# Norms between attention and feed-forward: VectorE and ScalarE steps in a written order, tiles in two pairs, fewer small steps

## The chip, the core and the metric

The kernel runs on one core of one Trainium2 chip. The metric is the device time of one execution in microseconds (us). Before the change it is 681.78 us, the median of 3 runs (680.45 to 683.81).

## What is computed

One layer of a decoder on a sequence of 512 tokens of width 1024: a token mixer (differential attention and sparse attention side by side), then a SwiGLU channel mixer, with an RMSNorm before and after each. The change is about the lines in the middle, between the output projection of the mixer and the two projections `w_gate` and `w_up`:

```python
def rms_norm(x, g):
    xf = x.astype(jnp.float32)
    y = xf * lax.rsqrt(jnp.mean(xf * xf, axis=-1, keepdims=True) + NORM_EPS)
    return (y * g.astype(jnp.float32)).astype(x.dtype)
...
        mix = hybrid_mixer(h, ...)              # ends with ... @ w_out
        x = x + rms_norm(mix, attn_post_norm[l])
        h = rms_norm(x, ffn_pre_norm[l])
        f = (jax.nn.silu(h @ w_gate[l]) * (h @ w_up[l])) @ w_down[l]
        x = x + rms_norm(f, ffn_post_norm[l])
```

## The kernel before

Everything is float32 in meaning; for TensorE each operand is split into a high and a low part of type fp32r, and each product is three products (high by high, low by high, high by low). The 512 tokens are four tiles of 128 rows, the partitions; a tile's 1024 columns are two halves of 512. A PSUM tile of 128 x 512 is called a bank below.

**Up to the norms.** `mix_part` (L683) has computed the first half of the sum of the output projection into `mixp`, held in the buffers named `rope`. `mix_final` (L695) adds the second half in PSUM: tiles 0 and 1 (`mix0`, `mix1`) end with the last attention head, tiles 2 and 3 follow on TensorE at once, in banks of the tag "o" (four banks).

**The norms.** `norm_post(i, mix)` (L807) handles the norm after attention for tile i. For each half, VectorE adds the two partial sums (L811), GpSimd multiplies by the norm's weights (`u`, L812). `row_rsqrt` (L785) squares the halves on ScalarE with a running sum per row (L788), VectorE adds the two sums (L791), and `rsqrt_mean` (L126) makes the row's 1/sqrt: logarithm and exponential on ScalarE (L129, L130), then four steps of one number a row on VectorE (L131 to L138), a Newton step among them. Then VectorE adds `u` times that to the residual `x2[i]` (L815). `norm_pre(i)` (L819) norms `x2[i]` again for the feed-forward: the squares, the row's 1/sqrt, and the product with weights and 1/sqrt, for tiles 0 and 2 as a GpSimd product (L824) and a ScalarE one (L828), for tiles 1 and 3 as one VectorE instruction (L830); the string `PREE = "adad"` (L73) says which. TensorE transposes the result (L835, `trh`), ScalarE rounds it to `hth` (L838), VectorE makes the low part `htl` (L839).

**After the norms.** `ff_gate` (L890) multiplies two column blocks of `w_gate` and `w_up` by `hth` and `htl`, first for tokens 0 to 255 (tiles 0 and 1), then for tokens 256 to 511: 48 products of 256 columns for each of two blocks and each half, so 96 a half (`gu`, L897). A third block follows for all tokens (48 products of 512 columns). Each ends with Silu on ScalarE (L902) and a product on VectorE (L903). `h_sums_a`, `h_sums` and `h_split` (L856 to L881) form sums of the tiles, and `ff_prep` (L924) sums of the weights, for `ff_seven` (L956), which computes the other 19 blocks with seven half-size products each (`gw`, L917).

**Order of the work.** The program is written step by step, and a scheduler with its own model of time then orders each engine's queue; `tc.high_priority` moves a group forward, and `tc.issue_after` fixes one instruction behind another. Each engine works through its queue strictly in that order. The four `norm_post` and `norm_pre` groups are written one after the other with priorities `HP2` and `HP3`:

```python
    for i in range(NT):
        ...
        with tc.high_priority(offset=HP2 * (NT - i)):
            norm_post(i, mix if i > 1 else (mix0, mix1)[i])
        if i:
            with tc.high_priority(offset=HP3 * (NT - i + 1)):
                norm_pre(i - 1)
```

The last norm of the layer, at the end of the program, uses `row_rsqrt` too (L1239).

Of the kernel before, what the change touches and what calls it, by code (L numbers as in the profile page):

```python
# [84 lines left out]
def hybrid_block_kernel(  # L85
# [699 lines left out]
    def row_rsqrt(src, tag, also=None):  # L785
        ss = cpool.tile([P, 2], F32, tag="ss" + tag, name="ss", bufs=2)
        for c in range(2):
            act.activation(junk[tag], src[c], AF.Square, accum_out=ss[:, c:c + 1])  # L788
            if also and c == 0:
                also(c)  # L790
        dve.tensor_tensor(ss[:, 0:1], ss[:, 0:1], ss[:, 1:2], OP.add)  # L791
        r = cpool.tile([P, 1], F32, tag="rs" + tag, name="rs", bufs=2)
        rsqrt_mean(r, ss[:, 0:1], 1.0 / D_MODEL, tag)
# [10 lines left out]
    mixt, us = [None] * NT, [None] * NT
    hraw = [None] * NT

    def norm_post(i, mix):  # L807
        mixt[i], us[i] = big("mixt"), big("u", tag="t21")
        m, u, x_ = halves(mixt[i]), halves(us[i]), halves(x2[i])
        for c in range(2):  # L810
            dve.tensor_tensor(m[c], mix[c], mixp[2 * i + c], OP.add)  # L811
            pool.tensor_tensor(u[c], m[c], g_post[:, CS[c]], OP.mult)  # L812
        r = row_rsqrt(m, "a")
        for c in range(2):
            dve.scalar_tensor_tensor(x_[c], u[c], r, x_[c], OP.mult, OP.add)  # L815

    scaled = [None]

    def norm_pre(i):  # L819
        u, x_ = halves(us[i]), halves(x2[i])  # L820
        m = halves(mixt[i])
        if PREE[i] == "a":
            for c in range(2):
                pool.tensor_tensor(u[c], x_[c], g_pre[:, CS[c]], OP.mult)  # L824
        r = row_rsqrt(x_, "b")
        for c in range(2):
            if PREE[i] == "a":
                act.activation(m[c], u[c], AF.Copy, scale=r)  # L828
            else:
                scaled[0] = dve.scalar_tensor_tensor(m[c], x_[c], r, g_pre[:, CS[c]], OP.mult, OP.mult)  # L830
        tr = wide(TRH[i], "trh")
        for c in range(2):
            for k in range(4):
                kk = 4 * c + k
                pe.transpose(tr[c][:, k * P:(k + 1) * P], mixt[i][:, kk * P:(kk + 1) * P], ident)  # L835
            tv = tr[c].rearrange("p (k t) -> p k t", t=P)
            d_h, d_l = (t[:, 4 * c:4 * c + 4, i * P:(i + 1) * P] for t in (hth, htl))
            act.activation(d_h, tv, AF.Copy)  # L838
            dve.tensor_tensor(d_l, tv, f32(d_h), OP.subtract)  # L839
        trs[i] = tr  # L840


    sums, raw4, trs = [], [None, None], [None] * NT
# [148 lines left out]
    for i in range(NT):  # L992
        if i > 1:
            mix = wide("o", "mix")
            mix_final(i, mix, MIX_B, True, True)
        with tc.high_priority(offset=HP2 * (NT - i)):
            norm_post(i, mix if i > 1 else (mix0, mix1)[i])
        if i:
            with tc.high_priority(offset=HP3 * (NT - i + 1)):
                norm_pre(i - 1)  # L1000
    with tc.high_priority(offset=HP3):
        norm_pre(NT - 1)
# [331 lines left out]
```

## Time and profile before

| What | Value |
|---|---|
| Median of the runs | 681.78 us (680.45 to 683.81) |
| The profiled execution's own time | 681.76 us |
| Its span, first to last instruction | 680.0 us |
| TensorE (matmul) busy | 644.9 us, 95% of the span |
| VectorE busy | 562.7 us, 83% |
| ScalarE busy | 389.6 us, 57% |
| GpSimd busy | 82.2 us, 12% |
| Mean granted TensorE clock | 0.976 of full speed |

The profile is of one execution. Its own time is 0.02 us from the median, and 1.8 us of it lie outside the span. Its instruction names are those of the program (PE is TensorE, PEld its weight load, DVE VectorE, ACT ScalarE, POOL GpSimd); the line numbers are those of the kernel before. An engine's idle time counts only where another engine waits for it.

### The profile page before, as it was taken

What the parts mean: (1) busy time and instruction counts of PE and PEld (TensorE: products, weight loads), DVE (VectorE), ACT (ScalarE), POOL (GpSimd) and SP (SyncE); (2) the same over time, 40 slices, a digit from 0 to 9 for tenths busy, and PEclk for the clock granted to TensorE, in tenths of its full rate; (3) what the DMA queues carried; (4) which work ended last, traced back from release to release, by engine and by line L of the source; (5) the groups of instructions that cost most, each with busy time, mean ns of one, the idle gap of its engine ahead of it and who ended that gap; (6) DMA issues with size and microseconds to landing.
All of it is one profiled execution on the core that took longest, in us unless ns stands there. A gap on an engine that the chain in (4) does not pass through costs nothing.

```text
span 680.0 us, 11179 instructions
## 1 busy us (share of the span) xinstructions
PE 644.9 (95%) x4099; PEld 576.7 (85%) x4099; DVE 562.7 (83%) x1122; ACT 389.6 (57%) x820; POOL 82.2 (12%) x90
## 2 busy tenths in 40 slices
PE   9999999999899998797889999999999999999994
PEld 5988788999788787676888999999999998878883
DVE  4878797887999978768998988888888649999957
ACT  7443454658799768535654556566555547665522
POOL 0000000110745423306300000000000000000020
PEclk9999999999899998989789999999999999999998
DMA  8446758671131520154214232332323216562533
GB/s 304 157 140 222 282 201 302 245 263 48 45 96 33 160 105 16 65 175 164 94 33 153 94 125 94 106 113 103 114 94 125 95 47 247 199 230 76 207 64 124
DMA packets 29735, 94.50 MB, mean 139 GB/s; under 512 B 3824, under 2 KB 4720, under 8 KB 28784
## 3 DMA queue, kind: packets, MB, share of 16 engines
q1 hardware_dynamic: 29104, 92.74, 39.1%
q0 software_dynamic: 576, 1.05, 0.9%
q8 instruction: 32, 0.52, 0.3%
q14 instruction: 23, 0.19, 0.1%
HBM read 80.66 MB, written 12.06 MB: 136 GB/s over the span
## 4 chain that ended last, share of the span: by engine, by line
PE 79%; DVE 9%; ACT 5%; DMA 4%; issue 2%; POOL 1%; SPq 0%; DVEq 0%; ACTq 0%
PE gw L917 28%; PE acc L1136 16%; PE fm L294 10%; PE gu L897 5%; PE dv L368 3%; PE mixp L688 3%; PE tr L513 3%; PE avn L641 2%; PE vg L390 2%; DMA wraw<-in_wf 2%; PE sc L497 2%; ACT p L503 2%; PE sc L498 1%; DVE p L502 1%; DMA gain<-in_grow 1%
## 5 line engine op out<-in xcount | busy, mean ns | idle before, releaser
L522 POOL TENSOR_TENSOR p<-p,l 128x384 f32<-128x384 f32 (+3 forms) x60 | 49.2, 847 | 130.4 <-DVE l L552 57.4
L503 ACT ACTIVATE p<-p,nm 128x128 f32<-128x128 f32 (+1 forms) x96 | 53.2, 556 | 15.5 <-DVE nm L502 14.9
L108 ACT ACTIVATE whi<-wraw 128x1024 fp32r<-128x1024 f32 (+2 forms) x36 | 37.1, 1037 | 43.4 <-PE fm L294 17.8
L118 DVE TENSOR_TENSOR wlo<-wraw,whi 128x1024 fp32r<-128x1024 f32 (+2 forms) x36 | 42.9, 1197 | 18.6 <-ACT whi L108 18.6
L502 DVE CUSTOM_DVE_ANT_0 p<-sc,mask_b 128x128 f32<-128x128 f32 (+1 forms) x96 | 43.8, 483 | 6.6 <-PE sc L498 5.9
L1218 POOL DMA_DIRECT2D rope<-dp x4 | 3.7, 1129 | 318.7 <-DVE rope L1213 318.7
L518 DVE TENSOR_TENSOR ptl<-tr,pth 128x384 fp32r<-128x384 f32 (+1 forms) x60 | 35.6, 595 | 5.9 <-ACT pth L517 5.2
L517 ACT ACTIVATE pth<-tr 128x384 fp32r<-128x384 f32 (+1 forms) x60 | 31.0, 518 | 16.3 <-PE tr L513 15.8
L513 PE MATMUL tr<-ident,p 128*128 128x128 f32 x200 | 34.7, 292 | 3.5 <-DVE rr L131 2.2
L497 PE MATMUL sc<-kst,qst 128*128 128x128 f32 (+2 forms) x96 | 33.7, 359 | 3.8 <-DVE nm L502 2.9
L294 PE MATMUL fm<-xh,whi 128*128 128x512 f32 x128 | 33.5, 396 | 1.5 <-ACT whi L108 1.4
L294 PE MATMUL fm<-xh,wlo 128*128 128x512 f32 x128 | 32.6, 391 | 0.0
L513 PEld LDWEIGHTS tr<-ident,p 128*128 128x128 f32 x200 | 25.4, 150 | 8.4 <-DVE ptl L518 2.7
L294 PE MATMUL fm<-xl,whi 128*128 128x512 f32 x128 | 32.3, 390 | 0.0
L498 PE MATMUL sc<-kst,qst 128*128 128x128 f32 (+2 forms) x96 | 31.1, 327 | 0.0
L294 PEld LDWEIGHTS fm<-xh,whi 128*128 128x128 f32 x128 | 23.6, 188 | 7.3 <-ACT whi L108 2.1
L294 PEld LDWEIGHTS fm<-xl,whi 128*128 128x128 f32 x128 | 24.0, 188 | 5.0
L294 PEld LDWEIGHTS fm<-xh,wlo 128*128 128x128 f32 x128 | 23.8, 188 | 4.8
L497 PEld LDWEIGHTS sc<-kst,qst 128*128 128x128 f32 x96 | 18.6, 194 | 7.6 <-DVE nm L502 6.1
L1044 ACT ACTIVATE ah<-ff 128x256 fp32r<-128x256 f32 (+1 forms) x28 | 14.3, 512 | 14.5 <-DVE ff L1044 11.1
L917 PE MATMUL gw<-rope,whi 128*128 128x256 f32 x160 | 21.9, 279 | 0.0
L972 DVE TENSOR_TENSOR cy<-gw,cy 128x512 f32<-128x512 f32 x19 | 13.0, 684 | 10.7 <-PE gw L917 10.7
(352 smaller groups left out, 2051.2 us busy)
## 6 DMA issues: line engine op xcount, KB each, us to landing
wraw<-in_wg SPq DMA_DIRECT2D x22, 512.0 KB, 3.2
dr<-in_wd SPq DMA_DIRECT2D x22, 512.0 KB, 3.3
wu<-in_wu SPq DMA_DIRECT2D x19, 512.0 KB, 3.2
wraw<-in_wf SPq DMA_DIRECT2D x16, 512.0 KB, 4.5
qk<-rope SPq DMA_DIRECT2D x7, 1024.0 KB, 4.9
kst<-qk SPq DMA_DIRECT2D x24, 256.0 KB, 3.9
qst<-qk SPq DMA_DIRECT2D x16, 256.0 KB, 2.9
wraw<-in_wo SPq DMA_DIRECT2D x8, 512.0 KB, 3.7
```

The costliest lines, as they stand in the source:

```text
L108: act.activation(dst, src, AF.Copy)
L118: (lo_eng or dve).tensor_tensor(lo[:, :w], raw[:, :w], f32(hi[:, :w]), OP.subtract)
L294: pe.matmul(pt, w[:, k * P:(k + 1) * P], xx[k], start=(n == 0), stop=(n == 3 * NK - 1))
L497: pe.matmul(sv, lhs, kk[:, 0, :w], start=True, stop=False)
L498: pe.matmul(sv, lhs, kk[:, 1, :w], start=False, stop=True)
L502: dve.tensor_tensor_reduce(pt, sv, mask_b[:, (NT - 1 - i) * P:], -1.0, BIG, OP.add, OP.min, nm)
L503: act.activation(pt, pt, AF.Exp, bias=nm, scale=-1.0, accum_out=l[:, i:i + 1])
L513: pe.transpose(tr[:, n * P:(n + 1) * P], pts[i][:, j * P:(j + 1) * P], ident)
L518: dve.tensor_tensor(ptl[:, sl], trv, f32(pth[:, sl]), OP.subtract)
L522: pool.tensor_tensor(p, p, l.to_broadcast(list(p.shape)), OP.mult)
L917: m = pe.matmul(pt, ww[:, k * P:(k + 1) * P], hx[k], start=(start and n == 0), stop=(n == 11), skip_group_check=True)
L1136: m = pe.matmul(pt, x, y, start=(start and n == 0), stop=(stop and n == 2), skip_group_check=True)
```

## The change

The norms are no longer written as two functions with priorities, but as a list of steps, `STEPS`, which is read from left to right. A step is a letter, the tile, and mostly the half. Capital letters belong to the norm after attention, small ones to the norm before the feed-forward: M the sum of the two parts, U the weights' product (`/p` on GpSimd, `/d` on VectorE), Q and q a square, B and b a first small step, L and l logarithm and exponential, F and f three small steps, X the residual, w the product with weights and 1/sqrt (`/s`: one VectorE instruction), t the transposes, h and o the high and the low part. `q` places each VectorE and each ScalarE instruction behind the one before it on the same engine, so that these two engines' queues follow the list; TensorE and GpSimd are still ordered by the scheduler.

Four more things change. All four tiles use the one-instruction form of the last product, so GpSimd and ScalarE lose theirs for tiles 0 and 2. Of the eight products U, four move from GpSimd to VectorE (tiles 1 and 3). A norm has four small VectorE steps, all of the kind tensor_scalar, in place of five, of which two were tensor_tensor: the first half's sum goes into the bias of the logarithm, and the factor comes out as minus the 1/sqrt, so the residual is kept with its sign reversed. And the transposes of tiles 1 and 3 use the banks "gu", the first four gate blocks the banks "o". The last norm of the layer uses the same small steps, and its product with the weights becomes a scalar_tensor_tensor with factor -1.

```diff
-PREE = "adad"
-TRH = ("tr", "gu", "tr", "tr")
+TRH = ("tr", "gu", "tr", "gu")
+STEPS = (
+    "M00 Q00 M01 Q01 U00/p U01/p M10 M11 Q10 B0 L0 Q11 U11/d F0 U10/d X00 q00 X01 B1 L1 q01 F1 b0 X10 l0 "
+    "q10 X11 q11 f0 w00/s t00 w01/s t01 b1 l1 h00 h01 f1 w10/s t10 h10 w11/s o00 t11 h11 M20 M30 o01 o10 "
+    "Q20 M21 Q21 U20/p o11 U21/p M31 Q30 B2 L2 Q31 U31/d F2 X20 q20 X21 U30/d B3 q21 L3 F3 b2 l2 X30 X31 "
+    "q30 q31 f2 w20/s t20 w21/s t21 b3 l3 h20 f3 h21 w30/s t30 o20 w31/s t31 o21 h30 h31 o30 o31 "
+)
...
     def row_rsqrt(src, tag, also=None):
-        ss = cpool.tile([P, 2], F32, tag="ss" + tag, name="ss", bufs=2)
...
+        rr = cpool.tile([P, 8], F32, tag="rr" + tag, name="rr", bufs=2)
+        m, v, y, t, r, _, s0, s1 = (rr[:, j:j + 1] for j in range(8))
...
+                dve.tensor_scalar(m, s0, 4.0 / D_MODEL, 4.0 * EPS, OP.mult, OP.add)
...
+        act.activation(y, s1, AF.Ln, bias=m, scale=4.0 / D_MODEL)
+        last_exp[0] = act.activation(y, y, AF.Exp, scale=-0.5)
+        dve.tensor_scalar(v, s1, 4.0 / D_MODEL, m, OP.mult, OP.add)
+        dve.tensor_scalar(t, y, y, v, OP.mult, OP.mult)
+        dve.tensor_scalar(r, t, -3.0, y, OP.add, OP.mult)
...
+    def q(eng, op, *a, **k):
+
+        with ExitStack() as es:
+            if eng in row_of:
+                es.enter_context(tc.issue_after(row_of[eng]))
+            r = getattr({"a": act, "d": dve}[eng], op)(*a, **k)
+        r = r[-1] if isinstance(r, tuple) else r
+        row_of[eng] = getattr(r, "ins", r)
+        return r
...
+        elif k == "U":
+            a = halves(us[i])[c], halves(mixt[i])[c], g_post[:, CS[c]], OP.mult
+            pool.tensor_tensor(*a) if opt == "p" else q("d", "tensor_tensor", *a)
...
+        elif k == "X":
+            x_ = halves(x2[i])[c]
+            q("d", "scalar_tensor_tensor", x_, halves(us[i])[c], columns(i, "a")[4], x_, OP.mult, OP.subtract)
+        elif k == "w":
+            h, x_, r = halves(mixt[i])[c], halves(x2[i])[c], columns(i, "b")[4]
+            if opt == "s":
+                q("d", "scalar_tensor_tensor", h, x_, r, g_pre[:, CS[c]], OP.mult, OP.mult)
...
-    ff_gate(0, w0, 0, 256, "gu")
+    ff_gate(0, w0, 0, 256, "o")
     ff_gate(1, w1, 0, 256, "o")
...
     ff_gate(0, w0, 256, SEQ, "o")
-    ff_gate(1, w1, 256, SEQ, "gu")
+    ff_gate(1, w1, 256, SEQ, "o")
...
-        r = row_rsqrt(uh, "c", lambda c: dve.tensor_tensor(gh[c], uh[c], g_ffn[:, CS[c]], OP.mult))
+        r = row_rsqrt(uh, "c", lambda c: dve.scalar_tensor_tensor(gh[c], uh[c], -1.0, g_ffn[:, CS[c]], OP.mult, OP.mult))
...
-            dve.scalar_tensor_tensor(gh[c], gh[c], r, x_[c], OP.mult, OP.add)
+            dve.scalar_tensor_tensor(gh[c], gh[c], r, x_[c], OP.mult, OP.subtract)
```

**What moves, at three places.** Up to the first step of the norms the five queues stand as before.

VectorE, from the first tile's last norm steps on. `mixt` is a tile of the norm (in the change 3656, 3665, 3737 and 3740 for tiles 0 to 3; before 3604, 3626, 3706 and 3784), `rr`, `rs` and `ss` are the small steps' columns, `x2_1` the residual of tile 1. Before:

```order
L815 SCALAR_TENSOR_TENSOR x2_1_3593<-u_3627,rs_3636,x2_1_3593 128x512 x2
L811 TENSOR_TENSOR mixt_3706<-mix_3680,rope_2906 128x512
L791 TENSOR_TENSOR ss_3650<-ss_3650 128x1
L131 TENSOR_SCALAR rr_3655<-ss_3650 128x1
L791 TENSOR_TENSOR ss_3728<-ss_3728 128x1
L131 TENSOR_SCALAR rr_3733<-ss_3728 128x1
L811 TENSOR_TENSOR mixt_3706<-mix_3681,rope_2906 128x512
L133 SCALAR_TENSOR_TENSOR rr_3657<-rr_3656,rr_3655 128x1
L133 SCALAR_TENSOR_TENSOR rr_3735<-rr_3734,rr_3733 128x1
L137 TENSOR_SCALAR rr_3657<-rr_3657 128x1
L137 TENSOR_SCALAR rr_3735<-rr_3735 128x1
L138 TENSOR_TENSOR rs_3654<-rr_3656,rr_3657 128x1
```

And in the change:

```order
L974 TENSOR_SCALAR rr_3681<-rr_3681 128x1
L974 SCALAR_TENSOR_TENSOR x2_1_3593<-u_3666,rr_3669,x2_1_3593 128x512 x2
L974 TENSOR_SCALAR rr_3681<-rr_3681 128x1 x3
L974 SCALAR_TENSOR_TENSOR mixt_3656<-x2_0_3592,rr_3681,gain_3590 128x512 x2
L974 TENSOR_SCALAR rr_3695<-rr_3695 128x1 x4
L974 SCALAR_TENSOR_TENSOR mixt_3665<-x2_1_3593,rr_3695,gain_3590 128x512 x2
L974 TENSOR_TENSOR htl_3601<-trh_3703,hth_3600 128x4x128
L974 TENSOR_TENSOR mixt_3737<-mix_3604,rope_2906 128x512
L974 TENSOR_TENSOR mixt_3740<-mix_3630,rope_2906 128x512
L974 TENSOR_TENSOR htl_3601<-trh_3704,hth_3600 128x4x128
L974 TENSOR_TENSOR htl_3601<-trh_3723,hth_3600 128x4x128
L974 TENSOR_TENSOR mixt_3737<-mix_3605,rope_2906 128x512
```

Before, the sum of tile 2 (`mixt_3706<-mix_3680`) stood between the residual of tile 1 and the second norm of tiles 0 and 1; now all steps of tiles 0 and 1 come first, and the sums of tiles 2 and 3 stand between the low parts of tiles 0 and 1.

TensorE, from the last output projection to the first gate products (`trh` are the transposes, `gu` the gate banks). Before:

```order
L700 MATMUL mix_3759<-ws1_3099,oh7_3537 128x512
L835 MATMUL trh_3666<-ident_78,mixt_3604 128x128 x4
L835 MATMUL trh_3744<-ident_78,mixt_3626 128x128 x4
L835 MATMUL trh_3667<-ident_78,mixt_3604 128x128 x4
L835 MATMUL trh_3745<-ident_78,mixt_3626 128x128 x4
L897 MATMUL gu_3931<-hth_3600,ws0_3341 128x256 x4
L897 MATMUL gu_3932<-hth_3600,ws0_3351 128x256 x4
L897 MATMUL gu_3879<-hth_3600,whi_3329 128x256 x8
L897 MATMUL gu_3879<-htl_3601,whi_3329 128x256 x4
```

And in the change:

```order
L705 MATMUL mix_3631<-ws1_3099,oh7_3537 128x512
L1036 MATMUL trh_3703<-ident_78,mixt_3656 128x128 x4
L1036 MATMUL trh_3704<-ident_78,mixt_3656 128x128 x4
L1036 MATMUL trh_3723<-ident_78,mixt_3665 128x128 x4
L1036 MATMUL trh_3724<-ident_78,mixt_3665 128x128 x4
L870 MATMUL gu_3835<-hth_3600,whi_3329 128x256 x8
L870 MATMUL gu_3836<-hth_3600,whi_3335 128x256 x8
L870 MATMUL gu_3835<-htl_3601,whi_3329 128x256 x4
L870 MATMUL gu_3836<-htl_3601,whi_3335 128x256 x4
```

The transposes of tile 0 now stand whole before those of tile 1. The first two gate banks now are those that held the sums `mix_3604` and `mix_3605` of tile 2, so the first product into `gu_3836` needs VectorE's `mixt_3737<-mix_3605`.

ScalarE, from the last norm's logarithm to the last high part. Before:

```order
L788 ACTIVATE junkb_3603,ss_3838<-x2_3_3595 128x512 x2
L838 ACTIVATE hth_3600<-trh_3824 128x4x128
L129 ACTIVATE rr_3844<-ss_3838,eps_63 128x1
L838 ACTIVATE hth_3600<-trh_3825 128x4x128
L130 ACTIVATE rr_3844<-rr_3844 128x1
L902 ACT_TABLE_LOAD
L902 ACTIVATE ff0_3877<-gu_3879 128x256
L902 ACTIVATE ff1_3878<-gu_3931 128x256
L864 ACTIVATE s_3987<-trh_3824 128x512
L838 ACTIVATE hth_3600<-trh_3854 128x4x128
```

And in the change:

```order
L974 ACTIVATE junkb_3603,rr_3780<-x2_3_3595 128x512 x2
L974 ACTIVATE rr_3780<-rr_3780 128x1 x2
L974 ACTIVATE hth_3600<-trh_3787 128x4x128
L875 ACT_TABLE_LOAD
L875 ACTIVATE ff0_3833<-gu_3835 128x256
L875 ACTIVATE ff1_3834<-gu_3887 128x256
L974 ACTIVATE hth_3600<-trh_3788 128x4x128
L974 ACTIVATE hth_3600<-trh_3807 128x4x128
L974 ACTIVATE hth_3600<-trh_3808 128x4x128
```

The load of the Silu table and the first two Silus now stand between the first and the second high part of tile 2; before they stood behind both, and ahead of tile 3. On VectorE, in the same place, the change has the low part of tile 2 between the two last products of tile 3:

```order
L974 TENSOR_SCALAR rr_3780<-rr_3780 128x1 x4
L974 SCALAR_TENSOR_TENSOR mixt_3740<-x2_3_3595,rr_3780,gain_3590 128x512
L974 TENSOR_TENSOR htl_3601<-trh_3787,hth_3600 128x4x128
L974 SCALAR_TENSOR_TENSOR mixt_3740<-x2_3_3595,rr_3780,gain_3590 128x512
L876 TENSOR_TENSOR ff0_3833<-ff0_3833,gu_3836 128x256
L876 TENSOR_TENSOR ff1_3834<-ff1_3834,gu_3888 128x256
L974 TENSOR_TENSOR htl_3601<-trh_3788,hth_3600 128x4x128
L974 TENSOR_TENSOR htl_3601<-trh_3807,hth_3600 128x4x128
```

The last product of tile 3 (the second `mixt_3740<-x2_3_3595`) now needs `htl_3601<-trh_3787`, and with it the first transposes of tile 2.

## Rows read from the trace of the kernel before

**Rows 1.** The page, section 1: busy time, share of the span and instructions of each engine.

```profile
PE 644.9 (95%) x4099; PEld 576.7 (85%) x4099; DVE 562.7 (83%) x1122; ACT 389.6 (57%) x820; POOL 82.2 (12%) x90
```

**Rows 2.** Busy time of each engine in two stretches (start and end in us from the start of the span, length, then busy us and instruction count for PE, PEld, DVE, ACT and POOL; the last three columns are the granted TensorE clock as a share of full speed, the DMA share and GB/s).

```profile
316.40:349.08 32.68, 23.43 (x151) 21.66 (x149) 29.44 (x67) 19.04 (x49) 8.03 (x6) 0.79 0.22 81
...
368.78:460.00 91.22, 91.22 (x774) 91.21 (x773) 78.62 (x110) 51.63 (x91) 0.00 (x0) 1.00 0.31 105
```

**Rows 3.** TensorE in order of time up to 349 us: start us, us, engine, line, operation, out<-in, tile sizes, count, and in brackets the idle time before it with what ended that.

```profile
316.40 0.39 PE L700 MATMUL mix<-ws,oh 128*128 128x512 f32 x1
321.23 3.67 PE L835 MATMUL trh<-ident,mixt 128*128 128x128 f32 x16 [4.44 <-ACT mixt L828]
327.35 2.08 PE L897 MATMUL gu<-hth,ws 128*128 128x256 f32 x8 [2.44 <-ACT hth L838]
...
331.09 0.63 PE L897 MATMUL gu<-hth,ws 128*128 128x256 f32 x4
331.56 0.63 PE L897 MATMUL gu<-htl,ws 128*128 128x256 f32 x4
...
342.00 0.66 PE L835 MATMUL trh<-ident,mixt 128*128 128x128 f32 x4 [0.99 <-ACT s L864]
343.34 1.65 PE L897 MATMUL gu<-hth,whi 128*128 128x256 f32 x8 [0.69 <-ACT hth L838]
...
347.79 0.60 PE L835 MATMUL trh<-ident,mixt 128*128 128x128 f32 x4
```

**Rows 4.** TensorE in order of time from 349 us on, columns as in Rows 3.

```profile
363.18 2.03 PE L897 MATMUL gu<-hth,whi 128*128 128x512 f32 x8
365.05 2.03 PE L897 MATMUL gu<-htl,whi 128*128 128x512 f32 x8
...
368.78 0.63 PE L917 MATMUL gw<-hth,whi 128*128 128x256 f32 x4
```

**Rows 5.** Short stretches around the places where the clock of TensorE changes, columns as in Rows 2.

```profile
302.00:304.00 2.00, 1.15 (x5) 0.95 (x6) 1.19 (x3) 0.95 (x3) 0.00 (x0) 1.00 0.91 215
318.00:320.00 2.00, 0.00 (x0) 0.00 (x0) 1.97 (x8) 1.25 (x5) 1.12 (x2) 1.00 0.13 51
320.00:322.00 2.00, 0.77 (x4) 0.77 (x5) 2.00 (x7) 1.52 (x3) 0.36 (x1) 0.50 0.00 0
...
330.00:332.00 2.00, 2.00 (x18) 2.00 (x17) 1.91 (x9) 0.93 (x2) 0.00 (x0) 0.94 0.75 262
...
344.00:346.00 2.00, 2.00 (x11) 2.00 (x11) 2.00 (x5) 1.23 (x2) 0.00 (x0) 0.50 0.00 0
```

**Rows 6.** VectorE instructions of the norms between 304 and 343 us, by line and shape: count | busy us, mean ns of one | idle before.

```profile
L815 DVE SCALAR_TENSOR_TENSOR x<-u,rs,x 128x512 f32<-128x512 f32 x8 | 6.6, 871 | 0.2
...
L791 DVE TENSOR_TENSOR ss<-ss 128x1 f32<-128x1 f32 x8 | 4.6, 571 | 1.4 <-ACT junka L788 1.4
...
L138 DVE TENSOR_TENSOR rs<-rr 128x1 f32<-128x1 f32 x8 | 3.9, 496 | 0.1
L830 DVE SCALAR_TENSOR_TENSOR mixt<-x,rs,gain 128x512 f32<-128x512 f32 x4 | 2.8, 748 | 0.0
...
L131 DVE TENSOR_SCALAR rr<-ss 128x1 f32<-128x1 f32 x8 | 1.2, 151 | 0.2
```

**Rows 7.** VectorE in order of time, columns as in Rows 3.

```profile
304.56 0.69 DVE L811 TENSOR_TENSOR mixt<-mix,rope 128x512 f32<-128x512 f32 x1
...
311.00 0.22 DVE L133 SCALAR_TENSOR_TENSOR rr<-rr 128x1 f32<-128x1 f32 x1
...
317.09 1.09 DVE L791 TENSOR_TENSOR ss<-ss 128x1 f32<-128x1 f32 x1
...
344.57 0.67 DVE L863 TENSOR_TENSOR s<-hr,trh 128x512 f32<-128x512 f32 x1
345.16 0.68 DVE L943 TENSOR_TENSOR t<-wu,t 128x512 f32<-128x512 f32 x1
```

**Rows 8.** GpSimd in order of time, columns as in Rows 3.

```profile
305.33 5.05 POOL L812 TENSOR_TENSOR u<-mixt,gain 128x512 f32<-128x512 f32 x4 [23.16 <-DVE mixt L811]
...
316.90 1.26 POOL L812 TENSOR_TENSOR u<-mixt,gain 128x512 f32<-128x512 f32 x1 [1.96 <-DVE ss L791]
```

**Rows 9.** ScalarE in order of time, columns as in Rows 3.

```profile
310.43 0.29 ACT L129 ACTIVATE rr<-ss,eps 128x1 f32<-128x1 f32 x1 [1.19 <-DVE ss L791]
310.76 0.20 ACT L130 ACTIVATE rr<-rr 128x1 f32<-128x1 f32 x1
...
315.57 0.63 ACT L788 ACTIVATE junkb<-x 128x512 bf16<-128x512 f32 x1 [2.18 <-issue]
...
316.33 0.63 ACT L788 ACTIVATE junkb<-x 128x512 bf16<-128x512 f32 x1
...
335.23 0.60 ACT L838 ACTIVATE hth<-trh 128x512 fp32r<-128x512 f32 x1 [1.45 <-PE trh L835]
...
336.61 1.28 ACT L902 ACT_TABLE_LOAD   x1
337.90 0.39 ACT L902 ACTIVATE ff<-gu 128x256 f32<-128x256 f32 x1
```

**Rows 10.** VectorE in the last microseconds of the program, columns as in Rows 3.

```profile
674.35 0.15 DVE L131 TENSOR_SCALAR rr<-ss 128x1 f32<-128x1 f32 x1
...
675.24 1.41 DVE L1241 SCALAR_TENSOR_TENSOR ug<-ug,rs,x 128x512 f32<-128x512 f32 x2
```

More of the change, by code (lines that the diff above doesn't have):

```diff
@@ L785, in row_rsqrt @@
     def row_rsqrt(src, tag, also=None):
-        ss = cpool.tile([P, 2], F32, tag="ss" + tag, name="ss", bufs=2)
+        rr = cpool.tile([P, 8], F32, tag="rr" + tag, name="rr", bufs=2)
+        m, v, y, t, r, _, s0, s1 = (rr[:, j:j + 1] for j in range(8))
         for c in range(2):
[L788 to L793, printed above, removed]
+            act.activation(junk[tag], src[c], AF.Square, accum_out=(s0, s1)[c])
+            if c == 0:
+                dve.tensor_scalar(m, s0, 4.0 / D_MODEL, 4.0 * EPS, OP.mult, OP.add)
+                if also:
+                    also(c)
+        act.activation(y, s1, AF.Ln, bias=m, scale=4.0 / D_MODEL)
[3 more added lines that the diff above has]
+        dve.tensor_scalar(r, t, -3.0, y, OP.add, OP.mult)
         if also:
@@ L802, in halves @@
         return [t[:, sl] for sl in CS]
[L804 to L843, printed above, removed]
+    sums, raw4 = [], [None, None]
     def sum_alloc():
@@ L940, in split @@
             return hi, lo
-        dve.tensor_tensor(t1, b12, b11, OP.subtract)
+        with tc.issue_after(row_of["d"]):
+            dve.tensor_tensor(t1, b12, b11, OP.subtract)
         dve.tensor_tensor(t2, b22, t1, OP.subtract)
@@ L991, in hybrid_block_kernel @@
     w0, w1 = st["F0"], st["F1"]
[L992 to L1002, printed above, removed]
+    mixt, us, trs, rows = [None] * NT, [None] * NT, [None] * NT, {}
@@ new lines, in hybrid_block_kernel, with columns @@
+    row_of = {}
+    def q(eng, op, *a, **k):
[6 more added lines that the diff above has]
+        return r
+    mixes = [mix0, mix1]
+    for i in (2, 3):
+        mixes.append(wide("o", "mix"))
+        mix_final(i, mixes[i], MIX_B, True, True)
+    def columns(i, key):
+        if (i, key) not in rows:
+            t = cpool.tile([P, 8], F32, tag="rr" + key, name="rr", bufs=2)
+            rows[i, key] = [t[:, j:j + 1] for j in range(8)]
+        return rows[i, key]
@@ L1003, in hybrid_block_kernel @@
+    for tok in STEPS.split():
+        tok, _, opt = tok.partition("/")
+        n_step(tok, opt)
     x2d = dram.tile([NT, P, D_MODEL], F32, name="x2d")
@@ L1008, in hybrid_block_kernel @@
         ffr[f] = f32(sslot(f"ff{f}"))
-    ff_gate(0, w0, 0, 256, "gu")
+    ff_gate(0, w0, 0, 256, "o")
     ff_gate(1, w1, 0, 256, "o")
-    with tc.issue_after(getattr(scaled[0], "ins", scaled[0])):
+    with tc.issue_after(row_of["d"]):
         for i in range(2):
```

41 lines of the change are left out of this document (added).

## Prediction

> **What bounds the kernel now.** I read the page's busy shares first, then the busy times by stretch, then TensorE's own timeline, and last the queues that it waits for. TensorE is busy 95% of the span [rows 1]; from 368.78 us it does not pause [rows 2], so an earlier start there moves the end by as much. The exception is the stretch with the norms: between 316.4 and 349.08 it is busy 23.4 of 32.7 us at 0.79 of its clock [rows 2]. It stands idle from the last output projection until the first transposes (4.44 us before 321.23), again until the first gate product (2.44 before 327.35), and in small gaps around 342 [rows 3]. The waits are for ScalarE, which waits for VectorE's chain of norm steps.
>
> The idle time costs twice. [...] Around 342 two gaps of 0.99 and 0.69 us with four transposes between them are followed by 0.50 in 344 to 346 [rows 3, 5]; in 302 to 304 it is idle for 0.85 us, and the clock stays at 1.00 [rows 5]. At full clock four products of 256 columns take 0.47 us (331.09 to 331.56), eight of 512 take 1.87 [rows 3, 4]. So the gates need 192 x 0.1166 + 48 x 0.234 = 33.6 us, the 32 transposes at most 3.7 (half of 16 in 3.67 us at half clock, twice), together 37.3 [rows 3, 4]. From 316.4 to the first `gw` product at 368.78 pass 52.4 us: 15 us are lost, the most that this change can win.
>
> **Prices.** A VectorE product of 512 columns starts 0.60 us after the one before it [rows 7]; a scalar_tensor_tensor counts 0.67, two take 1.41 [rows 10]; a small step is 0.15, about 0.20 when the next one needs it [rows 6]. A square is 0.76 from one to the next [rows 9]; logarithm and exponential together take 0.57 until VectorE can go on (310.43 to 311.00) [rows 7, 9]; four transposes 0.60 [rows 3]; a high part 0.60 [rows 9]. A GpSimd product is 1.26 [rows 8].
>
> One price hides in the busy times. The small step L791 takes 571 ns on average, L138 496, other small steps 151 [rows 6]; the one at 317.09 ends at 318.18, as the GpSimd product that began at 316.90 ends (318.16) [rows 7, 8]. A VectorE instruction of two SBUF tensors waits for the running GpSimd product. That is 8 x 0.42 + 8 x 0.34 + 8 x 0.12 = 7.1 us (the last for L815, against L830's 748) that count as VectorE busy.
>
> **The change, part by part.**
>
> *VectorE's load.* It gains four products U (2.4 us) and four of the last product (4 x 0.748 = 3.0), and loses eight small steps (1.2) and most of the 7.1 us of waiting: GpSimd keeps four products, of which I charge 0.9 us again, U11 behind U01 and U31 behind U21. The new steps are tensor_scalar, which showed no such wait. Sum: 5.4 - 1.2 - 6.2 = -2.0 us.
>
> *Tiles 0 and 1.* I walk the written order. M00 starts as before at 304.56 [rows 7]; the four sums end at 307.1. U11 waits for GpSimd's second product (305.33 + 2 x 1.26 = 307.9), ends 308.5. Tile 0's factor is there at 308.9, U10 ends 309.5, the residual X00 and X01 310.9. B1, L1 and F1 give tile 1's factor at 312.05, X10 and X11 end 313.4, f0 313.9, w00 and w01 315.25. l1 starts after b1 at 315.45, f1 ends 316.45, w10 and w11 317.85. TensorE leaves the output projection as before; tile 0's transposes are then waiting for it, tile 1's last four start at 317.9, and ScalarE's four high parts end at 319.7, the two that come first in the product at 319.1. The first gate bank is free when M20 has read it, at 319.2. So the first gate product starts at **319.3 instead of 327.35**. After eight products the second bank is wanted, which M21 frees only at 321.6 (o01 and o10 stand before it): a wait of 1.45 us. The other 88 products take 10.3 us: 331.9 at full clock.
>
> *Tiles 2 and 3* start on VectorE with M31's end at 322.75. U31 ends 323.5, X20 and X21 325.45, U30 326.05, F3 327.25, X30 and X31 328.65, w20 and w21 330.45, f3 331.65, w30 332.35. Here the queues bind the engines to each other: w31 stands behind o20, which needs h20, which needs tile 2's transposes, and these stand on TensorE behind all first-half gates. And h21, h30 and h31 stand on ScalarE behind the table load (1.28 us) and two Silus (0.39 each, a little less in a row) [rows 9].
>
> *The clock.* Between 316.6 and 321.65 TensorE has only transposes and eight products, much like 341 to 343.3 before. I expect one fall here; its price is that of the fall around 344: from 343.34 to 347.79 sixteen products of 256 and four of 512 columns took 4.45 us instead of 2.80, so 1.65 [rows 3]. The first half then ends at 333.5; h20 ends 334.75, o20 335.4, w31 336.1; the table load and Silus end near 336.6, h21 at 337.2, h30 at 337.8. Second half from 337.8, a second fall for 1.65 us after this gap: 337.8 + 11.2 + 1.65 + 11.2 = **361.8** for the first `gw` product, 7.0 us earlier. Bounds: no fall at either gap gives 358.6 (-10.2); another 3 us of waits in the queues gives -4.0.
>
> *What follows `gw`.* VectorE must form sums and weight parts before it: about 21 us of its work after o31, which ends near 339, so 360; what comes last is wanted some 5 us after `gw` starts, and in the long stretch VectorE is busy 78.6 of 91.2 us [rows 2]. It fits, at nothing, with some 6 us to spare.
>
> *The last norm.* From L131 to the last product were 0.89 us in four steps [rows 10], now three at about 0.6; two scalar_tensor_tensor for tensor_tensor give 0.15 back. -0.1 us, between -0.4 and +0.2. The x2 and weight loads and the bank names cost nothing; each transfer is asked for earlier than before, as its buffer falls free earlier.
>
> Sum, against the profiled execution's own 681.76 us (the median is 681.78): 681.76 - 7.0 - 0.1 = **674.6 us**.
>
> **Rivals.**
>
> *The clock does not fall.* For it: 302 to 304 [rows 5]; transposes and products fill part of each gap. Against it: the fall around 344. 681.76 - 10.2 - 0.1 = 671.4 us. Chance 0.2.
>
> *The gain is given back.* `gw` starts early but its operands are late: if VectorE's 21 us stretch to 28 or more by waits for ScalarE, TensorE stands in the first `gw` blocks instead. Against it: ScalarE is busy 57% of the span [rows 1]. From 7 us of delay on it costs as much as it exceeds that; with 12 the time is 681.76 - 7.1 + 5 = 679.7. Chance 0.1.
>
> *The written order holds the clock down.* If TensorE stays at 0.50 through the whole first half, that half takes 20.5 us from 321.65 on, the second starts at 346.4, `gw` at 370.5: 681.76 + 1.7 = 683.5. Before, it recovered within 3 to 4 us of steady products. Chance 0.04.
>
> *VectorE is the bound, and slower.* It is busy 29.4 of 32.7 us in the stretch [rows 2]; if the 7.1 us were work and not waiting, the change would load it with 5.4 us more and take off 1.2, on the path: 681.76 + 4.2 = 686.0 us. It decides once less than 4.2 us of those 7.1 go away. [...] Chance 0.03.
>
> **How the numbers follow.** My forecast has 0.63 and lies between 672.7 and 677.8 (the bounds of its terms). The range takes in the first rival and part of the second: 670.8 to 678.8 leaves out under 0.2. A measurement of this kernel tells about 0.5%, 3.4 us, from no change. Faster by more: forecast and first rival, and a share of the second, 0.86. Within 0.5%: the rest of the second and the third, 0.11. Slower: 0.03.
>
> **What would show it.** Right: the first gate product near 319, a wait of 1 to 2 us after its first eight, the clock at 0.50 once after 321 and once after 337, L791 and L138's successors at 0.15 to 0.2 us, the first `gw` product at 360 to 363 and no pause behind it. Wrong: VectorE's last product of tile 1 after 320, the second half of the gates after 341, TensorE idle after the first `gw` product, or the end moving by less than the first `gw` product does.

## The result, and the profile after

The changed kernel takes 672.62 us (median of 4 runs, 672.11 to 674.7), the kernel before, run beside it, 681.89 us: ratio 0.9862, 95% interval 0.984 to 0.9885. The forecast was 674.6 in a range of 670.8 to 678.8. The profiled execution of after took 672.15 us, its span is 670.4.

The page's busy line, then the stretches of [rows 2] (the norms' 32.68 us from the last output projection on, then `gw`) and TensorE's clock by 2 us (second last but one column: PEclk):

```profile
PE 639.4 (95%) x4099; PEld 570.4 (85%) x4099; DVE 561.1 (84%) x1118; ACT 387.2 (58%) x816; POOL 71.4 (11%) x82
```

```profile
315.54:348.22 32.68, 29.15 (x225) 27.39 (x224) 30.78 (x64) 18.64 (x44) 2.61 (x2) 0.95 0.23 81
359.54:450.76 91.22, 91.22 (x774) 91.21 (x773) 81.85 (x116) 51.58 (x93) 0.00 (x0) 1.00 0.32 111
...
320.00:322.00 2.00, 2.00 (x20) 2.00 (x19) 2.00 (x4) 0.27 (x3) 0.97 (x2) 1.00 0.00 0
...
336.00:338.00 2.00, 2.00 (x11) 2.00 (x11) 2.00 (x5) 0.26 (x1) 0.00 (x0) 0.50 0.60 236
338.00:340.00 2.00, 2.00 (x16) 2.00 (x16) 2.00 (x4) 0.00 (x0) 0.00 (x0) 0.81 0.00 0
```

In the stretch that had room TensorE is now busy 29.15 us, where it was 23.43, at a clock of 0.95 instead of 0.79 [rows 2]. The clock falls once, behind 334, to 0.50 in 336 to 338; at the first gate product (320 to 322) it stays at 1.00. TensorE's own timeline, which answers to [rows 3, 4] (start, busy us, line, product, and in brackets the idle time ahead and what ended it):

```profile
315.77 1.03 PE L1036 MATMUL trh<-ident,mixt 128*128 128x128 f32 x8
317.59 1.32 PE L1036 MATMUL trh<-ident,mixt 128*128 128x128 f32 x8 [0.79 <-DVE mixt L974]
319.55 2.13 PE L870 MATMUL gu<-hth,whi 128*128 128x256 f32 x16 [0.64 <-ACT hth L974]
...
330.96 1.29 PE L1036 MATMUL trh<-ident,mixt 128*128 128x128 f32 x8
333.65 0.63 PE L1036 MATMUL trh<-ident,mixt 128*128 128x128 f32 x4 [1.41 <-DVE mixt L974]
334.91 0.71 PE L1036 MATMUL trh<-ident,mixt 128*128 128x128 f32 x4 [0.63 <-DVE mixt L974]
335.65 2.07 PE L870 MATMUL gu<-hth,whi 128*128 128x256 f32 x8
...
359.54 0.63 PE L890 MATMUL gw<-hth,whi 128*128 128x256 f32 x4
```

The idle 4.44 and 2.44 us of [rows 3] have shrunk to 0.79 and 0.64; there is now a second gap of 1.41 and 0.63 us between the halves of the gates. ScalarE's timeline in that gap (`hth` at 332.07 is h20, the three at 334.50 are h21, h30 and h31):

```profile
331.63 0.53 ACT L974 ACTIVATE rr<-rr 128x1 f32<-128x1 f32 x2 [1.52 <-DVE rr L974]
332.07 0.58 ACT L974 ACTIVATE hth<-trh 128x512 fp32r<-128x512 f32 x1
332.67 1.28 ACT L875 ACT_TABLE_LOAD   x1
333.96 0.66 ACT L875 ACTIVATE ff<-gu 128x256 f32<-128x256 f32 x2
334.50 1.75 ACT L974 ACTIVATE hth<-trh 128x512 fp32r<-128x512 f32 x3
```

**One mark for all executions.** The start of `M00`, VectorE's first sum, is 304.56 us before [rows 7] and 303.71 after, although no instruction ahead of it has changed. In the profiles of the twelve experiments it lies between 304.67 and 307.49. So the times in the table count from M00. "First gate", "second half" and "gw" are the starts of the first gate product, of the first product of the gates' second half and of the first `gw` product, "tail" is from the first `gw` product to the span's end, "falls" the gaps at which the clock went to 0.50.

| profile | first gate | second half | gw | tail | falls |
|---|---|---|---|---|---|
| before | 22.79 | 38.78 | 64.22 | 311.2 | first, second |
| after | 15.84 | 31.94 | 55.83 | 310.9 | second |
| the same once more | 15.84 | 31.93 | 55.57 | 310.8 | second |
| e1 no written order | 18.94 | (no gap) | 56.24 | 310.9 | first |
| e2 small steps alone | 20.68 | 36.65 | 63.30 | 310.8 | first, second |
| e3 U on GpSimd | 15.82 | 31.78 | 54.28 | 310.9 | none |
| e4 w on GpSimd | 16.45 | 33.37 | 57.16 | 310.9 | second |
| e6 w31 first | 15.85 | 32.92 | 56.98 | 310.9 | first, second |
| e7 early l3 | 16.22 | 31.27 | 53.89 | 314.6 | first |
| e8 bank late | 15.84 | 32.91 | 56.96 | 310.8 | first, second |
| e9 second gap fed | 15.84 | 32.92 | 55.42 | 312.6 | first |
| e11 early l3, cy ahead | 15.85 | 30.77 | 53.27 | 312.2 | none |
| e12 both gaps fed | 15.88 | 31.94 | 54.45 | 312.6 | none |
| e13 e11 with U on GpSimd | 15.83 | 30.92 | 53.54 | 312.2 | first |

Of the 9.6 us of span between the two profiles, 0.85 lie ahead of M00, 8.4 between M00 and `gw` (64.22 to 55.83), 0.36 behind.

### The profile page after: what moved, and what is told of

Same layout as the page of the kernel before. It is cut to its first block, busy times and chain, and to the rows that moved or that the text cites. A ratio compares the mean times of both kernels' runs of the same rounds, so it can differ in the third digit from the quotient of the medians.

```text
span 670.4 us, 11184 instructions
## 1 busy us (share of the span) xinstructions
PE 639.4 (95%) x4099; PEld 570.4 (85%) x4099; DVE 561.1 (84%) x1118; ACT 387.2 (58%) x816; POOL 71.4 (11%) x82
## 4 chain that ended last, share of the span: by engine, by line
PE 48%; DVE 4%; issue 1%; ACT 1%; DVEq 0%; ACTq 0%
PE gw L890 28%; PE acc L1181 16%; PE gu L870 4%; DVE mixt L974 1%; DVE rr L974 1%; DVE x L974 1%; DVE ug L1286 0%; DVE htl L974 0%; ACT junkb L974 0%; ACT rr L974 0%; DVE ug L1284 0%; DVE uf L1282 0%; PE trh L1036 0%; DVE ffl L1089 0%; DVE cy L946 0%
## 5 line engine op out<-in xcount | busy, mean ns | idle before, releaser
L518 PE MATMUL tr<-ident,p 128*128 128x128 f32 x200 | 32.9, 280 | 4.1 <-DVE rr L136 2.2
L518 PEld LDWEIGHTS tr<-ident,p 128*128 128x128 f32 x200 | 24.0, 143 | 9.2 <-DVE ptl L523 3.5
L299 PEld LDWEIGHTS fm<-xh,whi 128*128 128x128 f32 x128 | 23.6, 188 | 7.2 <-ACT whi L113 2.0
```

The source lines that it names most:

```text
L299: pe.matmul(pt, w[:, k * P:(k + 1) * P], xx[k], start=(n == 0), stop=(n == 3 * NK - 1))
L518: pe.transpose(tr[:, n * P:(n + 1) * P], pts[i][:, j * P:(j + 1) * P], ident)
```

## The experiments

All but e2 are the changed kernel with one edit each (e10 with none). Ratios are to the kernel before, run beside them.

**The same kernel once more** (e10), no edit.

> The changed kernel once more, as it is. Theory A (whether TensorE's clock falls at a gap differs between executions with the same gaps): first gate product 15.8 us after M00 as in the first profile, but gw 54.3 us after M00 if the clock falls at no gap, 55.4 with a fall at the first alone, 55.8 at the second alone, 57.0 at both; median of the runs 672 to 673.5. Rival B (the clock follows the gaps): one fall, at the second gap, gw 55.8 us after M00 again.

Measured: 673.25 us, 0.9867 (0.9847 to 0.9886). The clock behaved as in the first profile (one fall, to 0.50 in 336 to 338), so this run by itself bears out B; that A holds is shown by the others. Compare the lines of TensorE that open the first half, of this run and of e6, whose instructions up to there are the same, with the same gap ahead:

```profile
320.54 2.11 PE L870 MATMUL gu<-hth,whi 128*128 128x256 f32 x16 [0.63 <-ACT hth L974]
```

```profile
320.52 3.54 PE L870 MATMUL gu<-hth,whi 128*128 128x256 f32 x16 [0.63 <-ACT hth L974]
...
334.62 1.29 PE L1036 MATMUL trh<-ident,mixt 128*128 128x128 f32 x8 [0.23 <-DVE mixt L974]
337.59 1.89 PE L870 MATMUL gu<-hth,whi 128*128 128x256 f32 x8 [1.69 <-ACT hth L974]
```

The same sixteen products take 2.11 us in the one and 3.54 in the other. With the first gap as it is (0.8 and 0.63 us idle) the clock stayed at 1.00 in after, e3, e10 and e11 and fell to 0.50 in e6, e8, e9 and e13.

**The second bank's release later** (e8). Edit: `M20 M30 o01 o10 ... U21/p M31` becomes `M20 o01 o10 ... U21/p M30 M31`.

> The changed kernel with sum M30 moved behind o11, directly ahead of M31, so that the banks fall free in the order M20, M21, M30, M31 and the second gate bank is the one that M21 reads, as the prediction had it. Theory A (the mis-read bank is the whole first-gap error): TensorE stops 0.5 to 1.5 us after the first eight gate products, and more for the third and fourth bank; if the stop makes the clock fall as the prediction said, 2 to 3.5 us later in all, time 674.5 to 676; if it does not, 673 to 674. Rival B (a shorter first half is idle time in the second gap anyway, since tiles 2 and 3 are the bound): first half ends later but the second half starts where it does now, time 672.3 to 673.

Measured: 673.45 us, 0.9866 (0.9846 to 0.9886). TensorE did not stop at any bank, but the run does not test what it was made for: the scheduler put four more products for the first bank behind the first eight, and the clock fell (0.50 in 322 to 324), so that twelve products last from 320.78 to 323.31. M21 ends at 322.43; my estimate from four products in 0.47 us at full clock [rows 3] is that the twelve would have ended near 322.2 there and a wait of 0.2 us been left. Both falls came, as in e6, and second half and `gw` lie where e6 has them (32.91 and 56.96).

**TensorE fed in the second gap, and in both** (e9, e12).

```diff
+            for j in range({0: 12, 1: 5}[c] if i == 3 else 0):
+                pe.matmul(trs[3][1][:, 0:256], w_col(w0[0][0], 0), hth[:, 0, 0:256], ...)
```

(The edit also places the transposes of tiles 2 and 3 one behind the other on TensorE, in e12 those of all tiles.)

> The changed kernel with 12 products of 256 columns on TensorE between the transposes of tiles 2 and 3, and 5 between those of tile 3, into the bank that t31 overwrites: TensorE works on through the second gap (1.41 and 0.63 us idle now), nothing else changes. Theory A (the gap makes the clock fall, for 1.5 us): no stretch at 0.50 behind 336, gw 1.5 us earlier in an execution that shows the fall and as it is in one that does not (the kernel with all products U on GpSimd had the same gap and no fall), so 671.1 to 672.3 in the median. Rival B (the fall is due to something else, or the added products delay the transposes): 672.5 to 674.

> The changed kernel with products that nothing uses on TensorE in both gaps: 8 of 128 columns between the transposes of tiles 0 and 1, 6 of 128 behind those of tile 1, 12 and 5 of 256 around those of tile 3. Theory A (a fed gap keeps the clock): no stretch at 0.50 behind M00, first gate product 15.8 to 16.3 us after M00, gw 54.3 to 54.8; time 670.5 to 672. Rival B (a fall is not due to the gap): one or two falls as before; Rival C (the added products delay the transposes and the gates by as much as the clock gives): 672.5 or more.

Measured: e9 674.47 us, 0.987 (0.9851 to 0.989); e12 673.5 us, 0.987 (0.9855 to 0.9885). Neither time fits its theory A: e9 lies above both of its ranges, e12 in that of rival C, although its first gate came as early as in after. In none of the three fed gaps did the clock fall (1.00 from 326 to 352 in e9, from 312 to 352 in e12). That is what A says, but three are few: four of the eight first gaps above kept the clock unfed, and so did the second gap of e3. A fall now has its price: the first half of the gates lasts 11.41 us in after (319.55 to 330.96), 12.83 in e6 (320.52 to 333.35), so 1.42; from the second half to `gw` pass 22.50 us in e3, e9 and e11 and 23.64 to 24.06 in after, e10, e6 and e8, so 1.1 to 1.6. With both gaps fed `gw` comes at 54.45, 1.1 to 1.4 us earlier than in after and e10; but the time is not better, because TensorE then waits once behind `gw` and the tail is 1.7 us longer. In e9 that wait, and ScalarE's queue ahead of it, read:

```profile
376.82 1.23 PE L890 MATMUL gw<-rope,wh 128*128 128x256 f32 x8 [1.46 <-ACT cy L938]
...
374.92 1.06 ACT L911 ACTIVATE wh<-wraw 128x1024 fp32r<-128x1024 f32 x1 [0.95 <-PE gw L890]
...
376.40 0.36 ACT L938 ACTIVATE cy<-gw 128x256 f32<-128x256 f32 x1
```

and in after:

```profile
371.67 0.37 ACT L938 ACTIVATE cy<-gw 128x256 f32<-128x256 f32 x1
373.45 1.06 ACT L911 ACTIVATE wh<-wraw 128x1024 fp32r<-128x1024 f32 x1 [1.41 <-PE gw L890]
```

`cy` copies the `gw` bank, which frees it for TensorE. In after it stands ahead of the high part `wh`, in e9 behind it (e12 has the same wait of 1.46 us for `cy`): the scheduler has moved it. An early `gw` is not the reason, since in e9 `gw` is hardly earlier than in e10 (55.42 and 55.57), and e3 has it at 54.28 without a stop. The place of `cy` is the subject of e11.

**No written order** (e1). Edit: `q` issues without `tc.issue_after(row_of[eng])`.

> The changed kernel with all its instructions, but VectorE's and ScalarE's steps are placed by the scheduler again, in the order that it finds. It puts sums M20 to M31 of 0.6 us each ahead of products of tiles 0 and 1 that the first gate product waits for. Theory A (the fewer and moved instructions carry the gain, the written order is worth 1 to 4 us): first gate product 1 to 3 us later than 319.6, time 674 to 677. Rival B (the written order carries the gain, without it the norms take what they took before): first gate product at 325 or later, time 679 to 683.

Measured: 674.01 us, 0.9893 (0.9876 to 0.9911). Theory A, at the edge of its ranges. TensorE's lines show what the order is worth and what it is not:

```profile
321.08 1.32 PE L1034 MATMUL trh<-ident,mixt 128*128 128x128 f32 x8 [1.52 <-DVE mixt L972]
325.42 2.08 PE L870 MATMUL gu<-hth,whi 128*128 128x256 f32 x8 [3.03 <-ACT hth L972]
...
335.53 0.60 PE L1034 MATMUL trh<-ident,mixt 128*128 128x128 f32 x4
...
362.72 0.63 PE L890 MATMUL gw<-hth,whi 128*128 128x256 f32 x4
```

The first gate product comes 3.1 us later, but there is no second gap: tile 2's transposes find their place among the first half's products. TensorE is idle for 4.55 us ahead of the first gate product, where after has 1.43 and then 2.04 in the second gap: two thirds of what the written order saves at the first gap come back at the second. It earns 0.4 to 0.7 us at `gw` (each of the executions compared has one fall), and by the ratios about 0.3% of the time, with intervals that overlap.

**Small steps alone** (e2): the kernel before with the new `row_rsqrt` (in the last norm too) and `OP.subtract` behind it.

> The kernel before with only the new form of the row factor (the addend goes into the logarithm's bias, three tensor_scalar behind it, one step fewer, in all three norms); products and order as before. Theory A: each of four row factors ahead of the first gate product loses a step (0.2 us) and a wait for GpSimd's product (up to 0.76 us), but the wait moves on to the next instruction with two SBUF inputs; 1 to 2 us earlier, 679.5 to 681. Rival B (the waits for GpSimd do not move on, and the small steps alone carry most of it): 675 or less. Rival C (nothing of it on the path): 681.5 to 682.

Measured: 681.57 us, 0.9991 (0.9977 to 1.0006), not to be told from no change. By the time that is rival C (681.5 to 682). In the profile the first gate product is 2.1 us earlier from M00, `gw` 0.9, and the tail is 0.4 shorter, which is nearer to theory A; a single execution each, so the 0.9 is not shown to be the edit's.

**U on GpSimd** (e3). Edit: `U11/d U10/d U31/d U30/d` become `/p`, behind the sums.

> The changed kernel with all eight products U on GpSimd. VectorE loses four products, 2.4 us. Theory A (VectorE waits out GpSimd's running product): the residual products X00 and X20 wait for the end of four GpSimd products in a row, about 309.6 and 325.7 us, 0.4 and 1.1 us later than now; first gate product 0 to +0.5 us, time 672.6 to 674. Rival B (no such wait, VectorE's load is what counts): the gate starts 1.2 us earlier, the second half too, time 670.2 to 671.4.

Measured: 672.83 us, 0.9863 (0.9844 to 0.9882). Theory A by the time, and the first gate is where it was. VectorE's X00 and X01 in after:

```profile
309.20 1.41 DVE L974 SCALAR_TENSOR_TENSOR x<-u,rr,x 128x512 f32<-128x512 f32 x2
```

The same two, and GpSimd's four products, in e3:

```profile
310.49 2.78 DVE L974 SCALAR_TENSOR_TENSOR x<-u,rr,x 128x512 f32<-128x512 f32 x2
...
307.22 5.50 POOL L1002 TENSOR_TENSOR u<-mixt,gain 128x512 f32<-128x512 f32 x4 [23.66 <-DVE mixt L974]
```

The pair takes 2.78 us instead of 1.41, and ends at 313.27, 0.55 us after GpSimd's last product (307.22 + 5.50 = 312.72). So the wait of [rows 7, 8] is real, and ahead of the first gate it gives back what two products off VectorE save. X00 does not wait for all four products, as theory A had it: the pair would then have ended near 314.1 (312.72 + 1.41); that it is X01 that is held is my reading of it. Behind the second four no such loss is seen: the second half starts 0.16 us earlier (31.78 against 31.94). Most of the early `gw` at 54.28 is not the edit's doing: this execution had no fall (1.00 from 314 to 352).

**The last product by GpSimd and ScalarE** (e4). Edit: `w00/s w01/s w20/s w21/s` become `w.. /p` behind X, and `z..` (ScalarE).

> The changed kernel with the last product of tiles 0 and 2 as before: GpSimd multiplies by the norm weight as soon as the residual is there, ScalarE applies the row factor. VectorE loses four products of 0.7 us, ScalarE gains four of 0.6 us in the chain, GpSimd four of 1.3 us. Theory A (a wash: VectorE's 1.4 us a pair come back as waits for GpSimd's products at X10 and X30 and as ScalarE's queue, where the logarithm of tile 1 stands behind two scalings): time 672.2 to 674. Rival B (VectorE's load counts): 1 to 2 us faster, 670.5 to 671.6. Rival C (moving the last product to VectorE is the heart of the change): 676 or more.

Measured: 674.96 us, 0.9898 (0.9879 to 0.9917). Between A and C: `gw` is 1.3 to 1.6 us later than in after and e10 with the same fall.

**w31 ahead of o20** (e6). Edit: `t30 o20 w31/s t31 o21` becomes `t30 w31/s t31 o20 o21`.

> The changed kernel with w31 and the transposes t31 written ahead of the low part o20, as in the prediction w31 is held behind it. Theory A (the second half of the gates waits for ScalarE's high part h30, which stands behind h20, the table load, two Silus and h21, not for w31): t31 starts 0.7 us earlier, but the second half starts where it does now, 31.9 us after M00 within 0.2; time 672.3 to 673. Rival B (w31 is what holds the second half): it starts 0.6 to 0.7 us earlier, time 671.7 to 672.

Measured: 672.08 us, 0.9835 (0.9816 to 0.9855). The time lies between the two theories' ranges. By the profile theory A: the transposes of tile 3 come together, but TensorE then waits 1.69 us for ScalarE (the lines above), and the second half starts at 32.92, as in e8 with the same falls and the old place of w31. Why the ratio is the lowest of all I cannot show; its interval overlaps that of after.

**l3 and the Silus early** (e7), **and cy ahead of them behind `gw`** (e11), **and U on GpSimd** (e13).

```diff
-q30 q31 f2 w20/s t20 w21/s t21 b3 l3 h20 f3 h21 w30/s t30 o20 w31/s t31 o21 h30 h31 o30 o31
+q30 q31 f2 b3 l3 w20/s t20 w21/s t21 f3 h20 h21 w30/s t30 w31/s t31 o20 o21 h30 h31 o30 o31
```

The list shown is that of e11. In e7 it has two more marks, one between l3 and w20 where the first half's gates are written, and one behind w31 where their two VectorE products are. In e11 and e13 these products are held behind w31 by `tc.issue_after`, and the high parts of later weights behind the first `cy` of the round before. e13 also has all eight products U on GpSimd, as in e3.

> The changed kernel with ScalarE's end of the norms in another order: b3 and l3 (tile 3's last logarithm and exponential) ahead of w20, then the table load and the two Silus of the first half ahead of h20; on VectorE f3, w30 and w31 directly behind w21, the gate's two products and o20, o21 behind w31. Theory A (ScalarE's queue from l3 to h30 holds the second half, the table load now falls into its idle time): second half 30.7 us after M00 instead of 31.9, gw 1.2 us earlier, time 671 to 672; if the gap then is too short for the clock to fall, another 1.5 less, 669.5 to 670.5. Rival B (the first half's end and VectorE's products hold it): no change, 672.3 to 673.3.

> As the experiment with l3 and the Silus early, but the gate's two products are only held behind w31, and ScalarE's high part of a later weight piece is held behind the first copy of the gw bank (cy) of the round before, which stood behind it there. Theory A (the 3.3 us that TensorE stood in the gw blocks came from that place in ScalarE's queue): second half 31.3 us or less after M00, gw 52.9 to 54 us after M00, no pause behind it, the end 310.9 us after gw; time 669.5 to 671.5. Rival B (VectorE's weight parts are late whatever stands in ScalarE's queue, the gain is given back): TensorE pauses 1 us or more behind the first gw product, 672 or more.

> The kernel of the experiment with l3 early and cy ahead, with all eight products U on GpSimd: four products of 0.6 us less on VectorE, nothing else moved. Theory A (behind gw VectorE's work is the next bound, and the waits for GpSimd cost less than the four products): second half 30.8 us after M00, gw 53.0 to 53.6, the pause of 1.0 us in the gw blocks shrinks to under 0.5, time 670.5 to 672.2. Rival B (the waits for GpSimd give the products back): the pause stays 1 us, 672.5 to 674.

Measured: e7 676.05 us, 0.9897 (0.9878 to 0.9917); e11 672.73 us, 0.9857 (0.9843 to 0.9872); e13 672.89 us, 0.9851 (0.9828 to 0.9874). Up to `gw` theory A holds: the second half starts at 30.77 in e11 (in e7, with a fall at the first gap, at 31.27). In time it fails: e7 is slower than both of its theories, e11 and e13 have the time and the stop of their rivals B. In e7 TensorE stops twice behind `gw`; its line, and ScalarE's queue at the first stop:

```profile
367.26 1.21 PE L895 MATMUL gw<-rope,whi 128*128 128x256 f32 x8 [1.52 <-ACT cy L943]
...
365.36 1.06 ACT L916 ACTIVATE whi<-wraw 128x1024 fp32r<-128x1024 f32 x1 [1.74 <-issue]
366.32 0.61 ACT L916 ACTIVATE t4h<-t 128x512 fp32r<-128x512 f32 x1
366.84 0.36 ACT L943 ACTIVATE cy<-gw 128x256 f32<-128x256 f32 x1
```

The copy `cy` stands behind two high parts of later weights; the scheduler had put it ahead of the first of them in the changed kernel, and the edit of the norms moved it. In e11 that place is mended and one stop is left:

```profile
373.70 1.22 PE L893 MATMUL gw<-rope,wh 128*128 128x256 f32 x8 [1.00 <-ACT cy L944]
...
371.97 0.69 DVE L931 TENSOR_TENSOR t<-wraw,t 128x512 f32<-128x512 f32 x1
...
372.75 0.63 ACT L917 ACTIVATE t4h<-t 128x512 fp32r<-128x512 f32 x1 [0.84 <-DVE t L931]
373.28 0.37 ACT L944 ACTIVATE cy<-gw 128x256 f32<-128x256 f32 x1
```

Here `cy` waits behind `t4h` for VectorE's `t` (L931), which in this order stands behind two sums of the `gw` blocks. e13 takes four products off VectorE and keeps the stop (0.99 us): rival B there. So of the 2.3 to 2.6 us that e11 wins at `gw` over after and the run of the same kernel, 1.2 come from the earlier second half and the others from an execution without a fall; the tail gives 1.4 back, and the rest is within the measurement's uncertainty. None of the versions is shown to beat the changed kernel.

## Why the prediction was right

By its own steps, counted from M00 (304.56 in the prediction):

- *TensorE sets the end, and an earlier `gw` moves it.* Shown in after: no pause behind 359.54, the tail 310.9 us as before less the last norm. The median lies 2.0 us under the forecast, the profiled execution 2.5 (9.6 against 7.1 us of gain): 0.85 ahead of M00, where nothing was changed, which is luck; 1.4 up to `gw`; 0.26 in the tail. The forecast's own bounds were 672.7 to 677.8, so 672.62 lies at their lower edge, and on the side of the first rival. The bound 672.7 was not worked out: the prediction's own case without a fall gives 671.4. (Its sum, 681.76 - 7.0 - 0.1, is 674.7 when rounded.)
- *First gate product, 14.74 predicted, 15.84 measured.* The walk was right in order and 1.1 us short in prices. VectorE is 0.63 us late with tile 0's factor (4.97 against 4.34) and 1.2 with the last product of tile 1 (14.50 against 13.29). A small step counts 0.211 on average and three in a row 0.84, where I charged 0.15 to 0.20 each; between the first and the second of tile 0's three steps VectorE is idle for 0.46 us more:

```profile
L974 DVE TENSOR_SCALAR rr<-rr 128x1 f32<-128x1 f32 x32 | 6.6, 211 | 2.8 <-ACT rr L974 1.3 <-DVE rr L974 0.5
```

```profile
306.28 1.29 DVE L974 TENSOR_TENSOR u<-mixt,gain 128x512 f32<-128x512 f32 x1
307.50 0.20 DVE L974 TENSOR_SCALAR rr<-rr 128x1 f32<-128x1 f32 x1
308.16 0.52 DVE L974 TENSOR_SCALAR rr<-rr 128x1 f32<-128x1 f32 x2 [0.46 <-DVE rr L974]
...
313.22 0.84 DVE L974 TENSOR_SCALAR rr<-rr 128x1 f32<-128x1 f32 x3
...
318.72 1.28 DVE L974 TENSOR_TENSOR mixt<-mix,rope 128x512 f32<-128x512 f32 x2
...
321.11 0.68 DVE L974 TENSOR_TENSOR mixt<-mix,rope 128x512 f32<-128x512 f32 x1
...
304.48 2.55 POOL L1002 TENSOR_TENSOR u<-mixt,gain 128x512 f32<-128x512 f32 x2 [22.77 <-DVE mixt L974]
```

  U11 waits for GpSimd's second product as charged: it lasts 1.29 us, until 307.57, and GpSimd ends at 307.03. From tile 1's last product to ScalarE's last high part, which ends at 319.55, it took 0.5 us less than charged; but the first gate product waits for that last part, and I let it start with the first two.
- *A wait of 1.45 us for M21 behind the first eight products: wrong.* Sixteen products run on from 319.55. I, and the text ahead of the prediction, gave the second gate bank the place that M21 reads. The lines above say otherwise: M21 starts at 321.11 and ends at 321.79, when all sixteen products have started. M20 and M30, the two sums of 318.72, end by 320.00, ahead of the ninth product at 320.57; so the second bank can be the one that M30 reads, which stands ahead of M21 in the written order. That a block gets the bank that fell free next is my reading of it. What M21's bank would have cost stays open (e8).
- *A fall at the first gap for 1.65 us: half right.* It is not in after, and it came in four of the eight unedited first gaps; its price is 1.42. The rival "the clock does not fall" is thus a matter of the execution as much as of the change. With both falls (e6, e8) `gw` comes at 56.97 against 57.24 predicted, which is closer than the steps were: the missing wait of 1.45 us and the late first gate nearly cancel.
- *Second half at 33.24; measured 31.94, and 32.92 where the first fall came.* The missing wait and fall, 3.1 us, are partly eaten by the late first gate. That w31 is held behind o20 is true and costs nothing (e6); ScalarE's queue, with the table load and the Silus behind h20, is the holder (e11: 1.2 us earlier with them ahead of h20; l3 was moved ahead of w20 as well, and the two were not tried apart).
- *Second half to `gw`, 22.4 + 1.65; measured 22.50 without and 23.6 to 24.1 with a fall.* Right.
- *VectorE has some 6 us to spare behind the gates.* Enough for this change, since in after nothing stops, nor in e3, whose `gw` is 1.5 us earlier. Whether it is 6 is open: where there are stops (e7, e9, e11, e12, e13), the order of the queues holds `cy`, and four products less on VectorE do not shorten the stop (e13).
- *VectorE's load, -2.0 us:* 562.7 to 561.1 us busy [rows 1], so -1.6.
- *The last norm, -0.1 (between -0.4 and +0.2):* the tail is 0.36 us shorter in after and 0.4 in e2; the lower bound.
- *The rivals.* "Given back" did not happen in after and did in e7, 3.7 us of it. The written order did not hold the clock down (1.00 from 314 to 334 in after), and VectorE did not get slower (busy 562.7 us before, 561.1 after). Four products moved from VectorE to GpSimd and ScalarE cost 1.3 to 1.6 us at `gw` (e4), and four others moved to GpSimd won nothing in the time (e3).

What no run settles is how the 8.4 us share out. One part undone costs 0.4 to 0.7 (order), 1.3 to 1.6 (w), nothing (U), and the small steps alone bring 0.9 in one profile: together 2.6 to 3.2 at `gw`. The parts may stand in for each other, as in e1, where a later first half closes the second gap; going back to tiles one by one was not tried, nor were the new banks of the transposes and gates apart from the rest. So most of the 8.4 us is shown for the whole change only.
